# Hybrid diffusion step on one core: the Fourier product's exit from PSUM, its gate loads and weight sums, and the place of one product

## The chip, the cores and the metric

The kernel runs on one core of one Trainium2 chip. A core has five engines that run on their own instruction streams: TensorE (PE, matmuls), VectorE (DVE), ScalarE (ACT), GpSimd (POOL) and SyncE (SP, which here issues DMAs). The metric is the device time of the whole kernel in microseconds (us). Before the change its median is 1737.0 us over three runs (1736.28 to 1737.26).

## What is computed

One layer of a hybrid backbone over 1152 tokens: 128 of a context pass and 1024 of a denoising pass on a 16 x 64 grid, with 1024 channels and fp32 inputs. Cut to what the change touches, and then to what follows:

```python
h = rmsnorm(x, norm1_g) * (1.0 + scale1) + shift1
z = h @ w_in + b_in                      # columns: x_r, y_r, x_f (512), gates g_a and g_b
x_r = depthwise_conv(x_r, conv_w, conv_b)
rec = rglru_bidir(x_r, ...)              # per direction: r, i = sigmoid(...); a = exp(...);
                                         # b = sqrt(1 - a*a) * (i * x); h = scan(a, b)
out_a = (rec * gelu(y_r)) @ w_lru_out
out_b = fourier_mix(x_f) @ w_fnet_out    # real part of a DFT over positions and 64 group channels
mixed = (sigmoid(g_a) * out_a + sigmoid(g_b) * out_b) @ w_out
x = x + gate1 * mixed                    # then a second norm, SwiGLU and a final norm
```

Every product of fp32 numbers is made of three fp32r matmuls: both operands are split into a rounded high part and the rest, and high x high, high x low and low x high are summed in PSUM.

## The kernel before

The tokens lie along the free dimension. A weight step (`zstep`) is one 128-channel block of a product: 8 blocks of the contraction, three passes, three pieces of 384 columns, 72 matmuls. Its weights come in one DMA of 128 x 1024 into a raw tile (three exist), are split by an ACT cast (L207) and a DVE subtraction (L208), and are used by PE at L242. A list of steps is made by hand (L1301 to L1430); a loop (L1568 to L1597) runs them one after the other. For each step it issues the next step's own loads (`pre`), then weight DMAs and weight splits up to the step's own and `cap` further ones, the step's matmuls, then as many of the waiting background tasks as a running count of ACT's and DVE's work allows, and last the step's own work on its result (`post`, `after`). All engines take their instructions in the order of this recording, and SP its DMAs too, at most eight of them in flight.

The stages that matter here:

- Eight y_r steps, three of the sixteen gate products, then four heads. A head h is two x_r steps, a gate product, the four recurrence gates of block 2h (18 matmuls each, a sigmoid on ACT at L503), another gate product, and the four gates of block 2h + 1. A gate product ends in one sigmoid (L392) and a spill to memory by POOL (L393): the first eight make `sgb_d` (gates of the Fourier branch), the others `sga_d`. A block's recurrence is a list of background tasks: exponential (L527) and tanh (L530) on ACT, products on DVE and POOL (L533, L537, L540), square root on ACT (L543), scans on DVE, and a store of the result to `p_d`. Exponential, square root and sigmoid need different activation tables, so `ACT_TABLE_LOAD` stands between them. Z, the PSUM pool of these steps, has two buffers.
- x_f in two halves of 256 channels (216 matmuls each, L613 to L615), with a gate product between them. Each half leaves PSUM by five bias additions on DVE (L624).
- Four last gate products (`tail`), with the matmuls of the position DFT woven between their own (L647 to L731). `nyq_before` (L752 to L764), run at the second of them, clears a tile on POOL, loads the weights for the Nyquist row and splits them.
- The Fourier product (`ob_steps`), eight blocks m in two parts each. Weight blocks are first summed (`ob_item`, L789 to L793). The even part's result is copied by ACT to `eb` (L823); the odd part adds to it in the same PSUM buffer, of which there are three. `post_o` then makes from both the direct rows (even plus odd) and the mirrored rows (twice even minus the whole), each at once multiplied with the gate tile `ld` read back from `sgb_d` (L771), and stores `gbob`.
- `oa`, the product with w_lru_out: 72 matmuls per step on p, which is read back from `p_d` (L871) and split by `p_tasks` into `phi` (ACT, L246) and `plo` (DVE, L247). The first of these steps is the first that needs all eight blocks of p.

Of the kernel before, what the change touches and what calls it, by code (L numbers as in the profile page):

```python
# [14 lines left out]
ALU = mybir.AluOpType  # L15
# [3 lines left out]
P = 128  # L19
D = 1024  # L20
KD = D // P
LAT = 1024
CTX = 128
# [5 lines left out]
NW = 33  # L29
NC = 34  # L30
C2 = 2 * NC
NF = 8 * NW + NC
# [27 lines left out]
def kernel(ctx: ExitStack, tc: tile.TileContext, xT, vecs, cbc, bfb, ada1, ada2, w_in, w_xf, gatew,  # L60
                         w_lru, w_fnet, w_fnq, w_out, w_uv, w_ff, w_ff2, dftc, dftx, identd, y_out, st_out):
    nc = tc.nc
    nc_v, nc_a, nc_p, nc_t, nc_s = nc.vector, nc.scalar, nc.gpsimd, nc.tensor, nc.sync
# [37 lines left out]
    def TT(name, dt=F32, shape=(P, T)):  # L101
        t = tp.tile(list(shape), dt, name=name, tag="T")
        held.append(t)
        return t

    def LL(name, shape=(P, T)):
        return lp.tile(list(shape), F32, name=name, tag="L")
# [13 lines left out]
    sgb_d = dr.tile([KD, P, T], F32, name="sgb_d")  # L121
# [77 lines left out]
    cost = {"A": 0.0, "D": 0.0}  # L199
# [28 lines left out]
    woven = []  # L228
# [354 lines left out]
    fx = {}  # L583
    F = {}
    fhi, flo = [None] * 4, [None] * 4
    nyq = {}
# [11 lines left out]
    def xf_step(hf):  # L598
        box = {}

        def pe(hl):
            zs = [Z(), Z()]
            box["zs"] = zs
            for t in range(9):
                weave()
                ps = zs[t // 6][:, (t % 6) // 2, (t % 2) * 256:(t % 2) * 256 + 256]
                for k in range(KD):
                    hl_k = hl[k // 4]
                    rh = hl_k[:, 0, (k % 4) * 256:(k % 4) * 256 + 256]
                    rl = hl_k[:, 1, (k % 4) * 256:(k % 4) * 256 + 256]  # L610

                    th, tl = hhi[k][:, t * P:(t + 1) * P], hlo[k][:, t * P:(t + 1) * P]
                    nc_t.matmul(ps, th, rh, start=(k == 0), stop=False)  # L613
                    nc_t.matmul(ps, th, rl, start=False, stop=False)
                    nc_t.matmul(ps, tl, rh, start=False, stop=(k == KD - 1))  # L615

        def post():
            xs = [TT(f"X{hf}{q}", shape=(P, 4, 256)) for q in range(3)]
            fx["X", hf] = xs
            bias = fx["dx"][:, None, 456 + 256 * hf:712 + 256 * hf]  # L620
            for t in range(0, 9, 2):
                n = 2 if t < 8 else 1
                z = box["zs"][t // 6][:, (t % 6) // 2, :n * 256].rearrange("p (a b) -> p a b", a=n)
                nc_v.tensor_add(xs[t // 4][:, t % 4:t % 4 + n, :], z, bias.to_broadcast([P, n, 256]))  # L624
            cost["D"] += 3.5
            box.clear()

        return Step(23.5, pe, post, [w_xf[hf, 0], w_xf[hf, 1]], before=xf_before if hf == 0 else None)


# [121 lines left out]
    def nyq_before():  # L752
        nyq["x"] = TT("nqx", F32R, (P, 2, NF))
        nyq["f"] = TT("nqf", F32, (P, 2, NF))
        nc_p.memset(nyq["f"][:72], 0.0)
        r = LL("nqr", (P, 1024))
        nc_p.memset(r[:72], 0.0)
        for o in (0, 32, 64):
            nc_s.dma_start(r[o:o + 8], w_fnq)
        w = nyq["w"] = TT("nqw", F32R, (P, 1024))  # L760
        nc_a.copy(w[:72], r[:72])
        nc_v.tensor_sub(w[64:72], r[64:72], w[64:72].bitcast(F32))
        cost["A"] += 1.1
        cost["D"] += 1.2  # L764


    lbox = {}

    def load_l(key, src, new=None):
        t = (new or LL)("ld")  # L770
        nc_s.dma_start(t[:], src)  # L771
        lbox[key] = t
# [26 lines left out]
    def ob_steps(m):  # L799

        box = {}

        def part(odd, hl):
            w = ob_op[m // 2]
            ps = box["ps"]
            for k in range(2):
                for i, (we, x_) in enumerate(((0, fhi), (0, flo), (1, fhi))):
                    o = (m % 2) * 512 + odd * 256 + k * P
                    for c in range(2):
                        nc_t.matmul(ps[:, c, :NF], w[:, we, o:o + P], x_[2 * k + odd][:, c, :],  # L810
                                    start=(not odd and k == 0 and i == 0), stop=(odd == 1 and k == 1 and i == 2),
                                    skip_group_check=odd == 1)

        def pe_e(hl):
            box["ps"] = G()
            part(0, hl)
            for c in range(2):
                nc_t.matmul(box["ps"][:, c, :NF], nyq["w"][:72, m * P:(m + 1) * P], nyq["x"][:72, c, :], start=False,
                            stop=True)

        def post_e():
            box["e"] = TT("eb", shape=(P, 2, NF))
            nc_a.copy(box["e"], box["ps"][:, :2, :NF])  # L823
            cost["A"] += 0.8

        def pe_o(hl):
            part(1, hl)
            if m % 2 == 1:
                del ob_op[m // 2]
            if m == KD - 1:  # L830
                fhi.clear()
                flo.clear()
                nyq.clear()

        def post_o():
            g = TT("gbob")
            s = lbox.pop(("sgb", m))
            ps, eb = box["ps"], box["e"]
            half = lambda t: t[:, :LAT].rearrange("p (h r w) -> p h r w", h=2, w=64)
            rows = lambda t: t[:, :2, :8 * NW].rearrange("p h (r w) -> p h r w", w=NW)  # L840
            ctx_ = lambda t: t[:, :2, 8 * NW:NF]
            n = LAT + C2
            d = TT("df", shape=(P, 16 * NW + C2))
            nc_v.scalar_tensor_tensor(d[:, :16 * NW].rearrange("p (h n) -> p h n", h=2), eb[:, :, :8 * NW], 2.0,
                                      ps[:, :2, :8 * NW], op0=ALU.mult, op1=ALU.subtract)
            nc_v.scalar_tensor_tensor(d[:, 16 * NW:].rearrange("p (h n) -> p h n", h=2), ctx_(eb), 2.0, ctx_(ps),
                                      op0=ALU.mult, op1=ALU.subtract)
            for h in range(2):
                nc_v.tensor_mul(half(g)[:, h, :, 0:NW], rows(ps)[:, h], half(s)[:, h, :, 0:NW])
            nc_v.tensor_mul(g[:, LAT:n].rearrange("p (h n) -> p h n", h=2), ctx_(ps),  # L850
                            s[:, LAT:n].rearrange("p (h n) -> p h n", h=2))
            dv = d[:, :16 * NW].rearrange("p (r w) -> p r w", w=NW)[:, :, 1:32]
            grid = lambda t: t[:, :LAT].rearrange("p (r w) -> p r w", w=64)
            g3, s3 = grid(g), grid(s)
            nc_v.tensor_mul(g3[:, 15:0:-1, 63:32:-1], dv[:, 1:16, :], s3[:, 15:0:-1, 63:32:-1])
            nc_v.tensor_mul(g3[:, 0:1, 63:32:-1], dv[:, 0:1, :], s3[:, 0:1, 63:32:-1])
            k = CTX - C2
            nc_v.tensor_mul(g[:, n:][:, ::-1], d[:, 16 * NW + 1:16 * NW + 1 + k], s[:, n:][:, ::-1])
            nc_p.dma_start(gbob_d[m], g[:])
            cost["D"] += 3.2  # L860
            box.clear()

        return (Step(1.95, pe_e, post_e, [ob_item(m), ob_item(m + 1)] if m % 2 == 0 else []),
                Step(1.65, pe_o, post_o, pre=lambda: load_l(("sgb", m), sgb_d[m], TT)))

    phi, plo = [None] * KD, [None] * KD

    def p_tasks():
        def f(k):
            t = TT("pl")  # L870
            nc_s.dma_start(t[:], p_d[k])  # L871
            lbox["p", k] = t

        def g(k):
            if k + 1 < KD:
                f(k + 1)
            phi[k] = TT(f"phi{k}", F32R)
            plo[k] = TT(f"plo{k}", F32R)
            split(lbox.pop(("p", k)), phi[k], plo[k], nc_a.copy)
        return [((lambda: f(0)), 0, 0)] + [((lambda k=k: g(k)), 1.2, 1.4) for k in range(KD)]  # L880


    mx = [[None] * KD, [None] * KD]
# [417 lines left out]
    steps = []  # L1301
# [5 lines left out]

    def g():
        return gs.pop(0)
    steps += [g() for _ in range(3)]  # L1310
    for hd in range(4):
        steps.append(zstep(w_in[2 * hd], xr_post, 2 * hd))
        steps.append(zstep(w_in[2 * hd + 1], xr_post, 2 * hd + 1))
# [6 lines left out]
    db = [dft_b(ct) for ct in range(4)]  # L1320
    dc = [[dft_c(pair, odd) for odd in range(2)] for pair in range(2)]
    one = lambda fs: [[f] for f in fs]
    steps += [xf0, g(), xf1]
    xf1.before = lambda: woven.extend(one(da[0] + da[1][:4]))
    tail = gs[:]
    gs.clear()
    tail[0].before = lambda: woven.extend([[da[1][4], db[0][0]]] + one(db[0][1:] + db[1] + da[2][:2]))
    tail[1].before = lambda: (nyq_before(), woven.extend(one(da[2][2:4]) + [[da[2][4], da[3][0]]] + one(da[3][1:4])
                                                         + [[da[3][4], dc[0][0][0]], [dc[0][0][1]]]))
    tail[2].before = lambda: woven.extend(one(dc[0][1] + db[2] + db[3]))  # L1330
    tail[3].before = lambda: woven.extend(one(dc[1][0] + dc[1][1]))
    steps += tail
# [1 line left out]
    ob[0][0].before = lambda: (open_pool("z", ("psg0", 3), space=PSUM), drain())  # L1334
    pt = [f for f, _, _ in p_tasks()]
    ob[5][0].after = pt[0]
    for m in range(KD):
        ob[m][0].cap = 2
        if m > 4:
            ob[m][1].after = pt[m - 4]  # L1340
    steps.append(ob[0][0])
# [356 lines left out]
```

## Time and profile before

| | |
|---|---|
| median of three runs | 1737.0 us |
| the profiled execution | 1734.3 us |
| its span, first to last instruction | 1732.2 us |
| mean granted TensorE clock | 0.981 |
| PE busy | 1654.1 us (95%) |
| DVE busy | 1029.3 us (59%) |
| ACT busy | 594.0 us (34%) |
| POOL busy | 115.8 us (7%) |

The span leaves out some 2 us of the execution that lie around the first and last instruction. Since PE is busy for 95% of it, the time hangs on the few places where PE stands still and on the clock behind them: the granted clock is 1.0 at 2.4 GHz and 0.5 at 1.2 GHz, and a figure between is the mean of a stretch. Positions in the trace are microseconds from the span's start.

### The profile page before, as it was taken

The page shows a single profiled execution, that of the slowest core. Times are in us where ns is not written, and L with a number is a line of the kernel's source. Part 1 is how long each engine was busy: PE and PEld are TensorE (multiplying, and loading weights), DVE is VectorE, ACT ScalarE, POOL GpSimd, SP SyncE. Part 2 cuts the span into 40 slices and gives each one's busy share as a digit, 9 for nine tenths or more (in the row PEclk, how much of TensorE's full clock was granted, in tenths as well). Part 3 has the DMA queues.
Part 4 walks back from the last instruction along what each step waited for, and adds up shares of the span by engine and source line. Part 5 has one row for each costly group of instructions (what it writes and reads, how often), then busy time and mean ns, then how long its engine had stood idle before and what let it go on. Part 6 is the DMA issues. An engine that isn't in the chain of part 4 may idle for free.

```text
span 1732.2 us, 25391 instructions
## 1 busy us (share of the span) xinstructions
PE 1654.1 (95%) x10680; PEld 1622.3 (94%) x10680; DVE 1029.3 (59%) x1466; ACT 594.0 (34%) x758; POOL 115.8 (7%) x161
## 2 busy tenths in 40 slices
PE   6899999899999899699998799999999999999997
PEld 4799999899999899699998799999999999999997
DVE  6678966798775225534456766555555566444446
ACT  6482225665572222311235422222222232111112
POOL 0200001101010000000000000000000000000012
PEclk9999999999999999899999899999999999999999
DMA  9038731322241106743433132222222227222203
GB/s 368 13 100 310 239 111 66 104 78 78 90 151 66 53 33 235 293 145 117 155 121 113 61 104 95 77 70 77 77 77 77 77 71 283 82 81 100 92 12 110
DMA packets 56481, 201.88 MB, mean 117 GB/s; under 512 B 6640, under 2 KB 9088, under 8 KB 56368
## 3 DMA queue, kind: packets, MB, share of 16 engines
q1 hardware_dynamic: 45776, 158.96, 27.2%
q0 software_dynamic: 10592, 41.30, 6.3%
q8 instruction: 84, 1.38, 0.3%
q14 instruction: 29, 0.24, 0.0%
HBM read 154.17 MB, written 46.01 MB: 116 GB/s over the span
## 4 chain that ended last, share of the span: by engine, by line
PE 65%; issue 6%; DVE 4%; ACT 2%; DMA 2%; POOL 0%; SPq 0%; DVEq 0%; ACTq 0%; POOLq 0%
PE g L933 31%; PE z L242 30%; PE z L1273 3%; DMA pl<-p_d 1%; DMA ld<-sgb_d 1%; ACT x L1015 0%; DVE x L968 0%; DVE x L1010 0%; DVE ho L1094 0%; ACT b L1022 0%; DVE tlo L247 0%; DVE yt L1296 0%; PE a L681 0%; ACT hl L207 0%; ACT hl L792 0%
## 5 line engine op out<-in xcount | busy, mean ns | idle before, releaser
L242 PE MATMUL z<-hhi,hl 128*128 128x384 f32 x1344 | 282.2, 341 | 0.0
L933 PE MATMUL g<-thi,ho 128*128 128x288 f32 x1408 | 251.4, 296 | 0.0
L242 PEld LDWEIGHTS z<-hhi,hl 128*128 128x128 f32 x1344 | 238.8, 189 | 0.8 <-issue 0.8
L933 PE MATMUL g<-b,ho 128*128 128x288 f32 x1584 | 222.3, 299 | 16.1 <-ACT w L1149 12.2
L933 PEld LDWEIGHTS g<-b,ho 128*128 128x128 f32 x1584 | 216.7, 191 | 17.3 <-ACT w L1149 12.9
L933 PEld LDWEIGHTS g<-thi,ho 128*128 128x128 f32 x1408 | 209.3, 189 | 0.0
L242 PE MATMUL z<-shi,hl 128*128 128x384 f32 x864 | 175.6, 338 | 0.9 <-DVE w L1179 0.9
L208 DVE TENSOR_TENSOR hl<-wr,hl 128x1024 fp32r<-128x1024 f32 x86 | 104.6, 1222 | 92.1 <-ACT hl L207 91.4
L207 ACT CAST hl<-wr 128x1024 fp32r<-128x1024 f32 x86 | 89.3, 1042 | 191.9 <-PE z L242 170.1
L242 PE MATMUL z<-hlo,hl 128*128 128x384 f32 x672 | 155.0, 339 | 0.0
L242 PEld LDWEIGHTS z<-shi,hl 128*128 128x128 f32 x864 | 153.7, 188 | 1.1 <-issue 1.1
L933 PE MATMUL g<-tlo,ho 128*128 128x288 f32 x704 | 151.3, 296 | 0.0
L242 PEld LDWEIGHTS z<-hlo,hl 128*128 128x128 f32 x672 | 121.2, 188 | 0.0
L1093 ACT CAST ho<-wr 128x512 fp32r<-128x512 f32 x110 | 64.6, 618 | 159.8 <-DVE wr L1103 141.9
L1094 DVE TENSOR_TENSOR ho<-wr,ho 128x512 fp32r<-128x512 f32 x110 | 75.4, 687 | 67.5 <-ACT ho L1093 67.5
L933 PEld LDWEIGHTS g<-tlo,ho 128*128 128x128 f32 x704 | 113.2, 189 | 0.0
L912 DVE SCALAR_TENSOR_TENSOR x<-z,mods,x 128x768 f32<-128x768 f32 x40 | 40.7, 1018 | 115.4 <-PE z L242 115.4
L933 PE MATMUL g<-mx,hl 128*128 128x288 f32 x768 | 101.6, 294 | 0.0
L933 PEld LDWEIGHTS g<-mx,hl 128*128 128x128 f32 x768 | 101.1, 188 | 0.0
L242 PE MATMUL z<-slo,hl 128*128 128x384 f32 x432 | 99.3, 338 | 0.0
L242 PE MATMUL z<-phi,hl 128*128 128x384 f32 x384 | 81.4, 348 | 13.0 <-DVE gbob L850 7.8
L242 PE MATMUL z<-xchi,hl 128*128 128x384 f32 x384 | 80.8, 342 | 7.9 <-ACT g L503 7.9
(256 smaller groups left out, 2519.9 us busy)
## 6 DMA issues: line engine op xcount, KB each, us to landing
wr<-in_w_uv_dram SPq DMA_DIRECT2D x50, 512.0 KB, 3.6
wr<-in_w_in_dram SPq DMA_DIRECT2D x32, 512.0 KB, 3.7
adar<-in_ada_dram SPq DMA_DIRECT2D x32, 512.0 KB, 5.1
s_d<-w POOLq DMA_DIRECT2D x44, 288.0 KB, 2.4
sld<-s_d SPq DMA_DIRECT2D x22, 576.0 KB, 4.8
wr<-in_w_ff_dram SPq DMA_DIRECT2D x22, 512.0 KB
ada<-in_ada_dram SPq DMA_DIRECT2D x16, 512.0 KB, 9.7
wr<-in_w_out_dram SPq DMA_DIRECT2D x13, 512.0 KB, 4.9
```

Of the source, the lines that this page charges most:

```text
L207: nc_a.copy(h[:, 0], r)
L208: nc_v.tensor_sub(h[:, 1], r, h[:, 0].bitcast(F32))
L242: nc_t.matmul(ps[:, c, :CH], w, xx[:, c * CH:(c + 1) * CH], start=(k == first and i == 0), stop=(k == last and i == 2))
L912: nc_v.scalar_tensor_tensor(dst[:, :768].rearrange("p (c n) -> p c n", c=2), ps[:, 0:2, :CH], mods[:, gq, 0, m:m + 1], src[:, :768].rearra ...
L933: nc_t.matmul(ps[:, c, :HC], w(e, k), xx[:, c * HC:(c + 1) * HC], start=(first and i == 0 and j == 0), stop=(last and i == len(ks) - 1 and ...
L1093: nc_a.copy(h[:, 0], src)
L1094: nc_v.tensor_sub(h[:, 1], src, h[:, 0].bitcast(F32))
L1273: nc_t.matmul(ps[:, b, :hi - lo], ww, xx[:, lo:hi], start=(j == js[0] and i == 0), stop=(j == js[-1] and i == 2))
```

## The change

It has four parts.

1. The list of steps begins with four gate products where it had three, and none stands between the halves of x_f any more. Three of a half's five bias additions are issued after its sixth group of matmuls, not after its last.
2. The Nyquist tile is cleared and loaded in `tail[0]`; its split becomes `nyq_weights`, woven in as the last piece of `tail[1]`.
3. `post_o` copies the direct rows from PSUM to `gbob` on ACT, makes the mirrored rows in `gbob` by five combinations on DVE, and multiplies the whole tile (1152 elements) with the gate tile in SBUF.
4. Gate loads are issued two to three blocks ahead, p loads two ahead, and `cap` is 4 at `tail[3]` and at the first two blocks (2 before).

```diff
+                if t == 5:
+                    out(range(0, 6, 2))
+        def out(ts):
+            if "X" not in box:
+                box["X"] = fx["X", hf] = [TT(f"X{hf}{q}", shape=(P, 4, 256)) for q in range(3)]
...
-            for t in range(0, 9, 2):
+            for t in ts:
...
+        def post():
+            out((6, 8))
...
-        r = LL("nqr", (P, 1024))
+        r = nyq["r"] = LL("nqr", (P, 1024))
         nc_p.memset(r[:72], 0.0)
         for o in (0, 32, 64):
             nc_s.dma_start(r[o:o + 8], w_fnq)
+
+    def nyq_weights():
+        r = nyq.pop("r")
         w = nyq["w"] = TT("nqw", F32R, (P, 1024))
...
-            s = lbox.pop(("sgb", m))
+            sb = lbox.pop(("sgb", m))
...
+            nc_a.copy(g[:, :LAT].rearrange("p (h r w) -> p h r w", h=2, w=64)[:, :, :, 0:NW], rows)
+            nc_a.copy(g[:, LAT:n].rearrange("p (h n) -> p h n", h=2), ps[:, :2, 8 * NW:NF])
+
+            g3 = g[:, :LAT].rearrange("p (r w) -> p r w", w=64)
+            for h, r0, r1, to in ((0, 1, 8, slice(15, 8, -1)), (1, 0, 8, slice(8, 0, -1)), (0, 0, 1, slice(0, 1))):
+                nc_v.scalar_tensor_tensor(g3[:, to, 63:32:-1], er[:, h, r0:r1, 1:32], 2.0, rows[:, h, r0:r1, 1:32],
+                                          op0=ALU.mult, op1=ALU.subtract)
+            gx = g[:, LAT:]
+            for h, a, b in ((0, 1, NC), (1, NC, CTX - C2 + 1)):
+                o = 8 * NW - h * NC
+                nc_v.scalar_tensor_tensor(gx[:, CTX - a:CTX - b:-1], eb[:, h, o + a:o + b], 2.0, ps[:, h, o + a:o + b],
+                                          op0=ALU.mult, op1=ALU.subtract)
+            nc_v.tensor_mul(g, g, sb)
...
-            if k + 1 < KD:
-                f(k + 1)
+            if k + 2 < KD:
+                f(k + 2)
...
-    steps += [g() for _ in range(3)]
+    steps += [g() for _ in range(4)]
...
-    steps += [xf0, g(), xf1]
+    steps += [xf0, xf1]
...
+    tail[3].cap = 4
+    ob[0][0].pre = lambda: sgb_load(0, 1, 2)
     for m in range(KD):
-        ob[m][0].cap = 2
+        ob[m][0].cap = 4 if m < 2 else 2
+        if 0 < m < 6:
+            ob[m][0].pre = lambda m=m: sgb_load(m + 2)
```

Part 1 also changes which background tasks the loop puts between the steps. On ACT, at head 1, before (`g_0_2160` and `g_2_2212` are the previous block's r of both directions, `g_0_2570` to `g_3_2653` the gates of this one):

```order
L392 ACT_TABLE_LOAD
L392 ACTIVATE sg<-z,vec 128x1152
L207 CAST hl<-wr 128x1024
L503 ACTIVATE g_0_2570<-z,vec 128x1152
L543 ACT_TABLE_LOAD
L543 ACTIVATE g_0_2160<-g_0_2160 128x1152
L543 ACTIVATE g_2_2212<-g_2_2212 128x1152
L503 ACT_TABLE_LOAD
L503 ACTIVATE g_1_2611<-z,vec 128x1152
L503 ACTIVATE g_2_2632<-z,vec 128x1152
L503 ACTIVATE g_3_2653<-z,vec 128x1152
```

and after, at the same head, with the gate product between its two blocks (`g_0_2671` and `g_2_2713` of the first block, `g_0_2870` to `g_3_2933` the gates of the second):

```order
L543 ACT_TABLE_LOAD
L543 ACTIVATE g_0_2671<-g_0_2671 128x1152
L543 ACTIVATE g_2_2713<-g_2_2713 128x1152
L392 ACT_TABLE_LOAD
L392 ACTIVATE sg<-z,vec 128x1152
L207 CAST hl<-wr 128x1024
L503 ACTIVATE g_0_2870<-z,vec 128x1152
L503 ACTIVATE g_1_2891<-z,vec 128x1152
L503 ACTIVATE g_2_2912<-z,vec 128x1152
L503 ACTIVATE g_3_2933<-z,vec 128x1152
```

The square roots (L543) moved from between two sigmoids of the gates to ahead of the gate product's sigmoid (L392); all four heads have the second form now, and before the last two had it.

On POOL, from the last store of p to the first stores of the Fourier product, before:

```order
L566 DMA p_d<-sq_4049 128x1152
L393 DMA sga_d<-sg 128x1152 x2
L755 MEMSET nqf 72x596
L757 MEMSET nqr 72x1024
L393 DMA sga_d<-sg 128x1152 x3
L859 DMA gbob_d<-gbob 128x1152 x8
```

and after (L761 and L763 are the same two lines):

```order
L566 DMA p_d<-sq_4130 128x1152
L761 MEMSET nqf 72x596
L763 MEMSET nqr 72x1024
L393 DMA sga_d<-sg 128x1152 x4
L864 DMA gbob_d<-gbob 128x1152 x8
```

The two clearings moved ahead of the spills of the tail's gate products, which wait for ACT.

On SP, around the Fourier product, before, from the first gate load on:

```order
L771 DMA ld<-sgb_d 128x1152 x2
L782 DMA wr<-in_w_fnet_dram 128x1024 x2
L771 DMA ld<-sgb_d 128x1152 x2
L196 DMA wr<-in_w_lru_dram 128x1024 x2
L771 DMA ld<-sgb_d 128x1152
L871 DMA pl<-p_d 128x1152
L771 DMA ld<-sgb_d 128x1152
L196 DMA wr<-in_w_lru_dram 128x1024 x2
L871 DMA pl<-p_d 128x1152
L771 DMA ld<-sgb_d 128x1152 x2
L871 DMA pl<-p_d 128x1152
```

and after, likewise:

```order
L780 DMA ld<-sgb_d 128x1152 x3
L791 DMA wr<-in_w_fnet_dram 128x1024 x3
L740 DMA nqf<-F 4x596 x3
L780 DMA ld<-sgb_d 128x1152
L791 DMA wr<-in_w_fnet_dram 128x1024 x2
L780 DMA ld<-sgb_d 128x1152 x3
L196 DMA wr<-in_w_lru_dram 128x1024 x2
L780 DMA ld<-sgb_d 128x1152
L881 DMA pl<-p_d 128x1152 x2
L196 DMA wr<-in_w_lru_dram 128x1024 x2
L881 DMA pl<-p_d 128x1152 x2
```

Seven of the eight gate loads moved ahead of the first w_lru load, where four stood, and p's first two loads ahead of the second pair of w_lru.

## Rows read from the trace of the kernel before

**Rows 1.** Waits of PE: engine, line, waited for: total us, times, longest
```profile
PE z L242 <- ACT g L503: 7.9, 2, 6.3
PE z L242 <- DVE gbob L850: 7.8, 1, 7.8
PE a L659 <- DVE u L652: 5.2, 1, 5.2
PE z L242 <- ACT phi L246: 5.2, 2, 4.0
```

**Rows 2.** Timeline of ACT, head 1: start, us, engine, line, instruction, idle before
```profile
321.85 2.43 ACT L543 ACTIVATE g<-g 128x1152 f32<-128x1152 f32 x2 [5.10 <-DVE g L540]
...
325.60 2.33 ACT L503 ACTIVATE g<-z,vec 128x1152 f32<-128x1152 f32 x2
```

**Rows 3.** Timeline of ACT, head 2, the gate product between its blocks
```profile
409.47 1.22 ACT L503 ACTIVATE g<-z,vec 128x1152 f32<-128x1152 f32 x1 [1.94 <-PE z L242]
...
422.36 1.28 ACT L392 ACT_TABLE_LOAD   x1
423.66 1.23 ACT L392 ACTIVATE sg<-z,vec 128x1152 f32<-128x1152 f32 x1
```

**Rows 4.** Timeline of PE, the same place
```profile
424.54 1.23 PE L242 MATMUL z<-xchi,hl 128*128 128x384 f32 x6
```

**Rows 5.** Windows: length, busy us (instructions) by engine, granted clock, DMA share, GB/s
```profile
326.87:331.56 4.69, 4.69 (x19) 4.69 (x19) 4.59 (x7) 1.06 (x1) 0.00 (x0) 0.66 0.00 0
607.78:614.75 6.97, 6.97 (x28) 6.97 (x29) 1.25 (x4) 0.77 (x2) 0.00 (x0) 0.60 0.00 0
650.00:660.00 10.00, 10.00 (x68) 9.70 (x68) 2.74 (x9) 1.77 (x3) 0.00 (x0) 1.00 0.05 21
710.00:720.00 10.00, 5.28 (x22) 3.81 (x20) 3.89 (x4) 1.15 (x1) 0.53 (x1) 0.79 1.02 419
```

**Rows 6.** Timelines of POOL, SP and ACT, the Nyquist weights
```profile
600.11 0.53 POOL L393 DMA_DIRECT2D sga_d<-sg  x1 [48.95 <-ACT sg L392]
...
601.16 0.98 POOL L757 MEMSET nqr<- 72x1024 f32 x1
...
602.17 1.04 SPq L759 DMA_DIRECT2D nqr<-in_w_fnq_dram  x3
...
605.02 1.04 ACT L761 CAST nqw<-nqr 72x1024 fp32r<-72x1024 f32 x1 [4.27 <-DMA nqr<-in_w_fnq_dram]
```

**Rows 7.** Timelines of DVE and PE, end of x_f's first half, last tail step
```profile
536.44 1.02 DVE L624 TENSOR_TENSOR X<-z,dx 128x512 f32<-128x512 f32 x2 [1.14 <-PE z L615]
537.38 2.35 DVE L208 TENSOR_TENSOR hl<-wr,hl 128x1024 fp32r<-128x1024 f32 x2
...
648.82 0.42 DVE L706 COPY F<-a 128x256 f32<-128x256 f32 x1
...
652.38 0.38 PE L702 MATMUL a<-dc,va 128*128 128x128 f32 x2
```

**Rows 8.** Groups by line, 665 to 730: count, busy us, mean ns, idle before
```profile
L247 DVE TENSOR_TENSOR plo<-pl,phi 128x1152 fp32r<-128x1152 f32 x8 | 10.8, 1356 | 7.6 <-ACT phi L246 7.4
...
L844 DVE SCALAR_TENSOR_TENSOR df<-eb,g 128x528 f32<-128x528 f32 x8 | 5.6, 698 | 1.9 <-PE g L810 1.9
...
L823 ACT COPY eb<-g 128x596 f32<-128x596 f32 x8 | 4.9, 652 | 0.0
```

**Rows 9.** Timelines of PE, SP and ACT, from the Fourier product to `oa`
```profile
665.30 0.43 PE L810 MATMUL g<-fhi,hl 128*128 128x298 f32 x2
...
706.17 4.60 SPq L871 DMA_DIRECT2D pl<-p_d  x4
...
724.35 1.15 ACT L246 CAST phi<-pl 128x1152 fp32r<-128x1152 f32 x1 [0.19 <-DMA pl<-p_d]
...
729.53 1.22 PE L242 MATMUL z<-phi,hl 128*128 128x384 f32 x6
```

**Rows 10.** DMA issues, 600 to 732: count, KB each, median us to landing
```profile
pl<-p_d SPq DMA_DIRECT2D x8, 576.0 KB, 13.9
```

More of the change, by code (lines that the diff above doesn't have):

```diff
@@ L615, in pe @@
                     nc_t.matmul(ps, tl, rh, start=False, stop=(k == KD - 1))
-        def post():
-            xs = [TT(f"X{hf}{q}", shape=(P, 4, 256)) for q in range(3)]
-            fx["X", hf] = xs
+                if t == 5:
[3 more added lines that the diff above has]
+                box["X"] = fx["X", hf] = [TT(f"X{hf}{q}", shape=(P, 4, 256)) for q in range(3)]
+            xs = box["X"]
             bias = fx["dx"][:, None, 456 + 256 * hf:712 + 256 * hf]
-            for t in range(0, 9, 2):
+            for t in ts:
                 n = 2 if t < 8 else 1
@@ L624, in post @@
                 nc_v.tensor_add(xs[t // 4][:, t % 4:t % 4 + n, :], z, bias.to_broadcast([P, n, 256]))
-            cost["D"] += 3.5
+                cost["D"] += 0.7
+        def post():
+            out((6, 8))
             box.clear()
@@ L836, in post_o @@
             g = TT("gbob")
-            s = lbox.pop(("sgb", m))
+            sb = lbox.pop(("sgb", m))
             ps, eb = box["ps"], box["e"]
-            half = lambda t: t[:, :LAT].rearrange("p (h r w) -> p h r w", h=2, w=64)
-            rows = lambda t: t[:, :2, :8 * NW].rearrange("p h (r w) -> p h r w", w=NW)
-            ctx_ = lambda t: t[:, :2, 8 * NW:NF]
             n = LAT + C2
-            d = TT("df", shape=(P, 16 * NW + C2))
-            nc_v.scalar_tensor_tensor(d[:, :16 * NW].rearrange("p (h n) -> p h n", h=2), eb[:, :, :8 * NW], 2.0,
-                                      ps[:, :2, :8 * NW], op0=ALU.mult, op1=ALU.subtract)
@@ L846, in post_o @@
[L846 to L858, printed above, removed]
+            rows = ps[:, :2, :8 * NW].rearrange("p h (r w) -> p h r w", w=NW)
@@ new lines, in post_o @@
+            er = eb[:, :, :8 * NW].rearrange("p h (r w) -> p h r w", w=NW)
+            nc_a.copy(g[:, :LAT].rearrange("p (h r w) -> p h r w", h=2, w=64)[:, :, :, 0:NW], rows)
[4 more added lines that the diff above has]
+                                          op0=ALU.mult, op1=ALU.subtract)
@@ L859, in post_o @@
+            gx = g[:, LAT:]
[4 more added lines that the diff above has]
+            nc_v.tensor_mul(g, g, sb)
             nc_p.dma_start(gbob_d[m], g[:])
-            cost["D"] += 3.2
+            cost["A"] += 0.9
+            cost["D"] += 2.7
@@ L861, in post_o, with sgb_load @@
             box.clear()
         return (Step(1.95, pe_e, post_e, [ob_item(m), ob_item(m + 1)] if m % 2 == 0 else []),
-                Step(1.65, pe_o, post_o, pre=lambda: load_l(("sgb", m), sgb_d[m], TT)))
+                Step(1.65, pe_o, post_o))
+    def sgb_load(*ms):
+        for m in ms:
+            load_l(("sgb", m), sgb_d[m], TT)
     phi, plo = [None] * KD, [None] * KD
@@ L879, in g @@
             split(lbox.pop(("p", k)), phi[k], plo[k], nc_a.copy)
-        return [((lambda: f(0)), 0, 0)] + [((lambda k=k: g(k)), 1.2, 1.4) for k in range(KD)]
+        return [((lambda: (f(0), f(1))), 0, 0)] + [((lambda k=k: g(k)), 1.2, 1.4) for k in range(KD)]
     mx = [[None] * KD, [None] * KD]
@@ L1326 @@
     gs.clear()
-    tail[0].before = lambda: woven.extend([[da[1][4], db[0][0]]] + one(db[0][1:] + db[1] + da[2][:2]))
-    tail[1].before = lambda: (nyq_before(), woven.extend(one(da[2][2:4]) + [[da[2][4], da[3][0]]] + one(da[3][1:4])
-                                                         + [[da[3][4], dc[0][0][0]], [dc[0][0][1]]]))
+    tail[0].before = lambda: nyq_before() or woven.extend([[da[1][4], db[0][0]]] + one(db[0][1:] + db[1] + da[2][:2]))
+    tail[1].before = lambda: woven.extend(one(da[2][2:4]) + [[da[2][4], da[3][0]]] + one(da[3][1:4])
+                                                         + [[da[3][4], dc[0][0][0]], [dc[0][0][1], nyq_weights]])
     tail[2].before = lambda: woven.extend(one(dc[0][1] + db[2] + db[3]))
```

## The prediction

> **What bounds the kernel now.** The page's first part gives TensorE (PE) 95% of the span, so I looked only for stretches in which PE waits, and took each for itself. The waits by engine come first [rows 1]; four entries lie in the part that the change touches. PE waits 7.9 us in two times, the longer 6.3, for a gate sigmoid; 7.8 us for the multiplication that frees a Fourier buffer; 5.2 us for a copy behind the Nyquist weights; 5.2 us for the fp32r casts of the recurrence's result p. The timelines say what stood ahead of each. Then the windows [rows 5] show what a wait costs behind its end: the granted clock is 0.66 in the 4.69 us after the first and 0.60 in the 6.97 us after the third, averages of a part at 1.2 GHz and a part at 2.4 GHz, each time after PE had stood still for over 5 us.
>
> **A. Four products first, halves of x_f in a row.** The step that stood between the halves moves ahead of the recurrence; its 72 matmuls are the same work. What changes is the order that the planner makes on ScalarE (ACT). Before, square roots stand between the first and the second sigmoid of a block's gates. At the first such place they wait 5.10 us for VectorE (DVE), so the second sigmoid starts only at 325.60, and PE waits with it [rows 2]. In the new order they stand ahead of the product's own sigmoid, and the four gate sigmoids follow each other. The old kernel has this order already at heads 2 and 3, so the trace shows its price: last gate sigmoid at 409.47, table load at 422.36, product's sigmoid from 423.66 to 424.89 [rows 3], and PE goes through the six matmuls at 424.54, three for each of two buffers, without a wait [rows 4]. The second three start some 0.53 us in, at 425.07: a margin of 0.2 us.
> Gone are then 7.9 us of wait [rows 1] and the slow clock behind the long one, 4.69 x (1 - 0.66) = 1.6 us [rows 5]: 9.5. The new order comes to two more places, heads 0 and 1. At head 1 the queues ahead are those of heads 2 and 3, so nothing is added. At head 0 DVE also has ten additions and products of eight elements ahead, at most the fixed 0.14 us each that the price in C gives [rows 8], so a stall between nothing and 1.4 - 0.2 us; I take 0.5. **A = -9.0** (ends -6 and -9.5).
> All of this goes by ScalarE's rows, where a table load is 1.28 us [rows 3]. The Trainium skill, page "ScalarE: Activation LUTs", section "Rules for kernel authors", tells to budget about 2.7 us for every switch to another set. The chain holds three switches (exponential, square root, sigmoid); each 1.4 us longer, it would be some 4.0 us late at each new place, A would be -9.5 + 8.0 = -1.5, and the sum 1719. The row speaks against it.
>
> **B. Nyquist weights.** PE's wait of 5.2 us [rows 1] ends a chain on three queues [rows 6]: GpSimd (POOL) clears the tile at 601.16, behind a spill that itself waited for ACT until 600.11; SyncE (SP) issues the three loads only at 602.17; ACT's cast starts at 605.02, and DVE's subtraction and copies follow. Now the clearing stands ahead of that spill, in the step before, and the loads with it, a whole product's time earlier; cast and subtraction are issued last among the woven pieces, behind the copies that PE waits for. What covers them is the rest of that step and the next. Gone: 5.2 + 6.97 x (1 - 0.60) = 2.8. **B = -7.9** (ends -8, and -6 if the two instructions still hold up a copy).
>
> **E. Second half's weights.** Without a step between the halves, the split of its second half-weight has no cover. In the trace DVE's last two bias additions begin at 536.44 upon PE's last matmul and take 1.02 us, and a subtraction is half of 2.35 [rows 7]; so the low part would be there about 2.2 us after the first half's end. PE asks for it 13 matmuls in, of 256 columns at the pace of [rows 4] (0.53 us for three of 384): 1.5 us. The change issues the other three additions within the half, which keeps them out of this chain. **E = +0.6** (0 to 2).
>
> **D. Last tail step.** With its look-ahead raised to 4, three weight sums are prepared ahead of the Fourier copies. The copy that started at 648.82 on DVE then stands behind three times two sums of 256 and a subtraction of 512 elements, 0.4 + 0.4 + 0.7 us by the price below, and ends near 653.2; PE's next group at 652.38 needs its buffer [rows 7]. **D = +0.8** (0 to 2).
>
> **C. From the Fourier product to the next stage.** S is the product's first matmul, 665.30; the last cast of p starts at 724.35, S+59, 0.19 us after its load, and the first p-step ends near 730.1, S+64.8, with the first three of the matmuls at 729.53 [rows 9]. DMA sets this end: in 710 to 720 the engines are busy 1.02 of the time at 419 GB/s, while in 650 to 660 they were busy 0.05 [rows 5]. The four last p loads were issued at 706.17 and over 4.60 us [rows 9].
> PSUM first. The product now leaves it by two ACT copies and five DVE combinations; the gate load is wanted only by one multiplication in SBUF. A DVE instruction costs 0.14 us plus 1.05 ns an element (0.698 us for 528, 1.356 for 1152 [rows 8]). Before: eight instructions, 1748 elements, 3.0 us a block. After: six, 1708 elements, 2.6 us. ACT gets some 0.6 + 0.25 us more a block, by its copy of 596 in 0.652 [rows 8], and DVE waits for it; three PSUM buffers hide that, but in the middle, where sums stand ahead, I count 1.5 us on PE. It replaces waits of the same size, so the stage stays at some 32 us. The 7.8 us go [rows 1], but PE then only comes to p earlier, and p's loads are late next.
> Loads next. Seven of eight gate loads stand ahead of the first w_lru load, in the idle stretch or right at S. SP then stops at the second w_lru load until a raw tile is free, behind the third block on DVE: an estimate of S+17, four blocks of 32 us / 8. From there to the last p load there are one gate load, eight of p, four for the next stage and five stores of 0.59 MB, and three weights of 0.52: 12.2 MB, 29 us at 419 GB/s, so S+46, and S+48.5 with the landing. ACT's cast and DVE's of 1.36 us [rows 8] and the rest of the matmuls give the first p-step's end at S+55.2. **C = -9.6.** Ends: -3 if SP is held some 7 us longer, -15 if the last load lands by S+43.
>
> **Sum.** -9.0 - 7.9 + 0.6 + 0.8 - 9.6 = -25.1. The profiled execution took 1734.3 us, which would become 1709.2; from the median of the runs, 1737.0, it is 1711.9.
>
> **Rivals.**
> 1. *The loads stay the bound.* The bytes are the same, the engines are full in the end, and the in-order SP queue can hold p behind w_lru. Against it: seven gate loads of 1.4 us each (0.59 MB at 419 GB/s) leave the full stretch. If it holds, C is -3: 1718.5.
> 2. *The recurrence's wait only moves.* The margin is 0.2 us, and head 0 has more on DVE. Each us on DVE is one of PE at two places; 3.5 us late at both gives A = -2.5: 1718.4. Against it: two places ran so without a wait [rows 4].
> 3. *More is won.* The last p lands by S+43: C = -15, 1706.5.
> 4. *Slower.* A task that casts p(k) issues the load of p(k+2), so two are ahead. If that ties issue to landing, the loads go in four pairs of 13.9 us [rows 10], the last landing at S+17 + 56 = S+73, 14 us later than before. With PE idle far longer, the first p-step runs at 1.2 GHz for another 5: C = +19, sum +3.5: 1740.5. It decides once landing and clock together are 15.5 us later than before. Against it: before, with one ahead, four loads were issued in 4.60 us [rows 9], so the issue did not follow the casts one by one.
> 5. *It does not do what it says*: the Nyquist wait stays because cast and subtraction come late all the same: 1719.8.
>
> **How the numbers follow.** Forecast 0.62, rivals 0.16, 0.08, 0.06, 0.06 and 0.02. A measurement here tells 0.2%, 3.5 us, from no change. Rivals 1 to 3 and 5 are all faster; of rival 4 I put a third within 0.2% (the pairs without the clock's loss, sum -1.5) and two thirds beyond: faster 0.94, same 0.02, slower 0.04. The range takes in the ends of A to E and rivals 1, 2, 3 and 5, and leaves out rival 4 and the corners where several ends meet: 1705 to 1724.
>
> **What will show it.** PE's waits for the gate sigmoid and for the copy at 602 gone, and the granted clock behind them at 1.0; the wait for the Fourier buffer (7.8) gone; last cast of p at about S+50; new waits of half a microsecond to one and a half at the second half of x_f, in the last tail step and in the middle of the Fourier product. Wrong would be a wait in heads 0 and 1 at the product's sigmoid, or a last p landing after S+56.

## The result, and the profile after

The changed kernel takes 1715.2 us (median of four runs, 1714.6 to 1717.9), the kernel before 1736.6 beside it: -21.4 us, ratio 0.9881 with a 95% interval of 0.9864 to 0.9898 (-18 to -24 us). Forecast were -25.1 us, 1711.9, within 1705 to 1724. A second measurement of both gave 0.9882. Seven single runs of the measurements below, one of them of the kernel before, were 9 to 13 us shorter than the median of the rest of their set, for no reason that was found; times are therefore medians, and the ratios, which such runs pull along, differ a little from them.

Where PE waits, by the waits of the changed kernel (engine, line, waited for: total us, times, longest), the entries that answer to [rows 1] and to the new waits of the forecast:

```profile
PE z L242 <- ACT phi L246: 5.1, 2, 3.0
...
PE z L242 <- DVE plo L247: 3.1, 4, 1.7
PE g L819 <- ACT eb L832: 2.5, 3, 1.7
...
PE z L242 <- DVE gbob L861: 1.2, 1, 1.2
...
PE a L708 <- DVE F L712: 0.8, 1, 0.8
...
PE z L242 <- ACT sg L392: 0.6, 1, 0.6
PE z L614 <- DVE hl L208: 0.3, 1, 0.3
```

The gate sigmoid's 7.9 us and the 5.2 behind the Nyquist weights have no entry any more; the Fourier buffer's 7.8 has become 1.2. The casts of p (phi and plo) now cost 8.2 us, where they cost 5.2 and 0.9 before: PE comes to them earlier and waits there.

The windows of the changed kernel (columns as in [rows 5]): head 0, the end of head 1, the tail steps with the Nyquist weights, the stretch from the end of SP's stop (SP standing at a weight load that waits for a free tile) to the last cast of p, and a window across the end of that stretch:

```profile
270.00:280.00 10.00, 9.39 (x54) 9.06 (x53) 9.89 (x9) 7.49 (x7) 0.00 (x0) 1.00 0.00 0
320.00:330.00 10.00, 10.00 (x59) 10.00 (x58) 9.74 (x9) 3.39 (x3) 1.00 (x2) 1.00 0.16 55
...
600.00:610.00 10.00, 10.00 (x73) 9.72 (x72) 3.08 (x8) 3.27 (x5) 0.00 (x0) 1.00 0.00 0
...
667.70:703.20 35.50, 24.18 (x134) 20.76 (x132) 24.77 (x43) 17.17 (x26) 2.67 (x5) 0.91 0.97 375
...
700.00:710.00 10.00, 8.18 (x32) 7.67 (x33) 4.59 (x4) 3.46 (x3) 0.00 (x0) 0.65 0.22 89
```

PE is full in 320 to 330 and 600 to 610, and the granted clock, 0.66 and 0.60 behind the two waits before [rows 5], is 1.00. What is left of the slow clock around here lies behind the waits for p: 0.84 in 690 to 700, 0.65 in 700 to 710.

To lay the traces side by side I use five marks in each: S, the Fourier product's first matmul; the last cast of p; the first post-operation of the next stage; the first matmul of the residual product; and that of the SwiGLU stage on the second half of the tokens. Times are us.

| kernel | S | S to last p cast | S to first post-operation | residual product to SwiGLU | median of runs |
|---|---|---|---|---|---|
| before | 665.3 | 59.1 | 65.0 | 164.7 | 1736.6 |
| after | 649.7 | 53.7 | 59.7 | 166.4 | 1715.2 |

Up to S the change wins 15.6 us, where A, B, E and D together had been put at 15.5. So close an agreement is luck: S lies between 649.0 and 651.2 in the eight traces, the changed kernel's among them, of kernels whose code up to S is that of the changed kernel, so one trace tells it to some 2 us. From S to the first post-operation the change wins 5.2 (64.96 against 59.74), where C had been put at 9.6. Then 1.7 are lost in a stretch that the change does not touch. In all the two traced executions differ by 19.0 us (1734.3 and 1715.3), the medians by 21.4; the executions of the kernel before counted so far lay between 1734.3 and 1737.3.

### The profile page after: what moved, and what is told of

It is laid out like the page before. It is cut to its first block, busy times and chain, and to the rows that moved or that the text cites. A ratio compares the mean times of both kernels' runs of the same rounds, so it can differ in the third digit from the quotient of the medians.

```text
span 1713.4 us, 25413 instructions
## 1 busy us (share of the span) xinstructions
PE 1650.7 (96%) x10680; PEld 1618.7 (94%) x10680; DVE 1029.1 (60%) x1450; ACT 598.2 (35%) x773; POOL 118.4 (7%) x161
## 4 chain that ended last, share of the span: by engine, by line
PE 75%; DVE 4%; issue 3%; ACT 2%; DMA 2%; POOL 0%; DVEq 0%; SPq 0%; POOLq 0%; ACTq 0%
PE z L242 35%; PE g L943 31%; PE z L1283 3%; DMA pl<-p_d 1%; PE z L614 1%; PE z L613 1%; PE z L615 1%; PE a L687 1%; PE g L819 0%; DVE hl L208 0%; ACT x L1025 0%; PE a L653 0%; DVE x L978 0%; DVE x L1020 0%; ACT b L1032 0%
## 5 line engine op out<-in xcount | busy, mean ns | idle before, releaser
L943 PEld LDWEIGHTS g<-b,ho 128*128 128x128 f32 x1584 | 217.5, 192 | 17.8 <-ACT w L1159 13.0
L421 DVE SCALAR_TENSOR_TENSOR junk<-adar,cb 128x1024 f32<-128x1024 f32 x64 | 78.3, 1224 | 5.0 <-DMA adar<-in_ada_dram 3.1
```

The source lines that it names most:

```text
L421: nc_v.scalar_tensor_tensor(env["j"], w, 1.0, env["c"][v], op0=ALU.mult, op1=ALU.mult, accum_out=out[:, v:v + 1])
L943: nc_t.matmul(ps[:, c, :HC], w(e, k), xx[:, c * HC:(c + 1) * HC], start=(first and i == 0 and j == 0), stop=(last and i == len(ks) - 1 and ...
```

## Experiments

The first question was whether the parts stand for themselves; the second, why C was half of what I had worked out.

### One part at a time

Part 1 alone is the kernel before with

```diff
-    steps += [g() for _ in range(3)]
+    steps += [g() for _ in range(4)]
...
-    steps += [xf0, g(), xf1]
+    steps += [xf0, xf1]
```

and the split bias additions. 

> Only part 1 on the kernel before: four gate products first, the halves of x_f in a row, three additions within the half. My theory (the gate sigmoids' wait and the clock behind it go, nothing takes their place): -9.5 +0.6 at head 0 +0.3 at the second half of x_f = -8.6, so 1728 for 1737; PE's waits for the gate sigmoid 0, one wait of some 0.6 for the product's sigmoid at head 0, granted clock 1.0 between 270 and 500. Rival (the wait only moves to the product's sigmoid at several heads): within 2 us of 1737, with waits of 3 us or more in two heads.

Measured: 1726.3 for 1734.8, ratio 0.9942 (0.9925 to 0.9958). S comes at 656.4, 8.9 earlier, and the stretch behind S is as before (65.1 for 65.0). PE's waits in heads and x_f are the two expected ones, 0.6 at the product's sigmoid of head 0 and 0.3 at the second half of x_f. The timeline of ACT in this kernel shows the 0.6:

```profile
270.83 2.44 ACT L543 ACTIVATE g<-g 128x1152 f32<-128x1152 f32 x2 [1.91 <-DVE g L540]
273.29 1.28 ACT L392 ACT_TABLE_LOAD   x1
274.59 1.22 ACT L392 ACTIVATE sg<-z,vec 128x1152 f32<-128x1152 f32 x1
```

At head 2 of the kernel before, the place that [rows 3] show, the square root waited 0.96 us for DVE:

```profile
419.90 2.44 ACT L543 ACTIVATE g<-g 128x1152 f32<-128x1152 f32 x2 [0.96 <-DVE g L540]
```

At head 0 it waits 1.91, so it is 0.95 later, and less the margin of 0.2 that is about the 0.6.

Part 2 alone:

```diff
-    tail[1].before = lambda: (nyq_before(), woven.extend(...
+    tail[0].before = lambda: nyq_before() or woven.extend(...
+    ... [dc[0][0][1], nyq_weights]
```

> Only part 2 on the kernel before: the Nyquist weights cleared and loaded one step earlier, split as the last woven piece. My theory: the wait of 5.2 and the slow clock behind it, 2.8, go together: -7.9, 1729; no wait at that place, clock 1.0 there. Rival (only the wait goes, the clock stays lower for another reason): -5.2, 1732. Rival (the split holds up the copies instead): under -3, 1734 or more.

Measured: 1728.0, ratio 0.9951 (0.9934 to 0.9969). S comes at 658.0, 7.3 earlier, though this execution was 0.7 late already when the heads ended (last gate matmul at 511.1 for 510.4), so the part won 8.0 in its place. No wait is left in 590 to 612 and the windows there show 1.00. Wait and clock went together.

Parts 3 and 4 alone, the new exit, loads and look-ahead. 

> Only parts 3 and 4 on the kernel before: the new exit from PSUM, the gate and p loads further ahead, more weight sums ahead. By the trace of the changed kernel its share is +0.8 at the last tail step and -5.2 from the Fourier product to the end of the first p-step: -4.4, 1732.6. By my blind forecast it would be -8.8, 1728. Rival (this stage gains only because its loads start later or earlier beside the other parts): between -2 and +2.

Measured: 1732.4, ratio 0.9977 (0.9964 to 0.9989), -2 to -6 us. From S to the first post-operation 59.3 for 65.0: the -5.2 of the changed kernel's trace does not hang on the other parts. The last tail step waits 0.8, as there. S itself comes 3.1 later in this trace (668.4); of that 1.5 stood already at the end of the heads, which this kernel leaves as they were, 0.8 is the wait, and the rest is open.

The changed kernel again. 

> The changed kernel again, for the sum of the three parts on the same chip: if the parts add up, -8.6 -7.9 -4.4 = -20.9, so 1716 for 1737; if they overlap, less than the three runs' sum by more than 3 us. Theory for the 1.7 us that the trace of the changed kernel loses between the first residual product and the SwiGLU products: chance of the clock's phase, so in this run between -1 and +2 against the kernel before; if it is an effect of the change, again 1.5 to 2.

Measured: 1714.5, ratio 0.9882 (0.9869 to 0.9895), -20.3 us. The three parts give -10.1, -8.5 and -4.0 by their ratios, -22.6 in sum, and -8.6, -6.8 and -2.4 by the medians, -17.8: the whole lies between. The stretch from the residual product to SwiGLU took 166.5 here. It also took 166.6 in the kernel with part 1 alone, whose code and neighbours there are those of the kernel before, and 165.9 with part 2 alone; over all thirteen later traces 165.0 to 166.8. So I take 164.7, of which there is one trace, as a short draw of the kernel before, and the 1.7 us as no effect of the change. What differs between draws was not tested.

### Exit or loads?

Two kernels each undo one side of what was done at the Fourier product. The first has the loads of before, and with them the look-ahead of before:

```diff
-                Step(1.65, pe_o, post_o))
+                Step(1.65, pe_o, post_o, pre=lambda: sgb_load(m)))
...
-            if k + 2 < KD:
-                f(k + 2)
+            if k + 1 < KD:
+                f(k + 1)
...
-    tail[3].cap = 4
...
-        ob[m][0].cap = 4 if m < 2 else 2
...
+        ob[m][0].cap = 2
```

> The changed kernel with the loads and look-ahead of before (gate loads block by block, p one ahead, look-ahead 2), and the new exit from PSUM kept. From the product's first matmul S to the first post-operation of the next stage: 65.0 before, 59.7 in the changed kernel. Theory (what the loads must carry after S sets that end): about 65, so 5 slower than the changed kernel, and 0.8 won back at the last tail step: some 1719. PE then comes to p early, but waits for p all the longer; no wait for the Fourier buffer. Rival (the exit itself gives the gain): about 60, some 1714.

The second has the `post_o` of before. 

> The changed kernel with the exit from PSUM of before (eight DVE instructions that read PSUM and the gate tile), and the new loads and look-ahead kept. Theory: the gate tiles are there in time, so the old exit does not hold PSUM; S to the first post-operation about 60, as in the changed kernel, total some 1714.5. Rival (the exit was needed): 65 or more, 1720.

Measured: 1720.9 (ratio 0.9921, 0.9897 to 0.9944) and 1715.6 (0.9888, 0.9867 to 0.9910). From S to the first post-operation:

| | loads and look-ahead of before | new loads and look-ahead |
|---|---|---|
| exit of before | 65.0 | 59.0 |
| new exit | 67.2 | 59.7 |

Loads and look-ahead together give all of it; which of the two gives how much is not shown, since no kernel undoes the look-ahead with the new loads kept. The new exit alone makes the stretch 2.2 longer: PE's waits with the old loads and the new exit are

```profile
PE z L242 <- ACT phi L246: 7.0, 3, 3.9
PE z L242 <- DVE plo L247: 4.6, 3, 3.7
PE g L819 <- ACT eb L832: 4.3, 4, 1.8
PE z L242 <- DVE gbob L861: 1.3, 1, 1.3
```

The 7.8 us of the Fourier buffer are gone without the new loads, but PE then stands before p, whose last cast comes at S+61.0 for S+59.1. With the new loads and the old exit that wait is 2.4 us and not 7.8:

```profile
PE z L242 <- ACT phi L246: 4.9, 2, 2.9
PE z L242 <- DVE plo L247: 2.8, 3, 1.6
PE z L242 <- DVE gbob L859: 2.4, 1, 2.4
PE g L819 <- ACT eb L832: 1.6, 2, 1.0
```

The gate tiles are there in time: DVE's multiplications of the direct rows stood idle 5.3 us for them in the kernel before, and not at all in this one (groups by line, before and this kernel):

```profile
L849 DVE TENSOR_TENSOR gbob<-g,ld 128x264 f32<-128x264 f32 x16 | 6.2, 427 | 5.3 <-DMA ld<-sgb_d 5.3
```

```profile
L858 DVE TENSOR_TENSOR gbob<-g,ld 128x264 f32<-128x264 f32 x16 | 6.1, 426 | 0.0
```

### What bounds the loads?

If C fell short because of the bytes that had to pass ahead of the last p load, then four loads that nobody needs yet should be moved behind it:

```diff
-    oa[0].before = lambda: ([f() for f in pt[4:]], open_pool(...
+    oa_pre = [oa[m].pre for m in range(2)]
+    oa[0].pre = oa[1].pre = None
+    oa[0].before = lambda: ([f() for f in pt[4:]], [f() for f in oa_pre], open_pool(...
```

> The changed kernel with the four loads of the next stage's first two steps (two gates, two Fourier products, 2.36 MB, 5.6 us at 419 GB/s) issued behind the last p load, not among them. Theory (bytes behind SP's stop): the last p cast starts at S+48 for S+53.5, the first post-operation at S+55 for S+59.7, so some 1710; the four loads then land about 6 us later, just in time for the two post-operations. Rival (the stop of SP and the order of casts set the end, not bytes): last cast at S+53 still, 1714.5. Rival (the four loads become late in turn): last cast early, first post-operation not, 1714.

Measured: 1707.6, ratio 0.9832 (0.9803 to 0.9861), 7 us under the changed kernel. Last cast at S+47.6, first post-operation at S+51.8 for S+59.7. That is 8 us for 5.6 us of bytes. The windows from S to that mark, of the changed kernel and of this one, show the rest:

```profile
649.70:709.40 59.70, 47.81 (x282) 44.15 (x282) 37.23 (x69) 25.72 (x40) 4.80 (x9) 0.91 0.78 299
```

```profile
651.00:702.70 51.70, 44.20 (x283) 41.23 (x282) 37.15 (x69) 25.62 (x40) 4.79 (x9) 1.00 0.89 343
```

The same matmuls kept PE busy for 47.8 us at a mean clock of 0.91 and for 44.2 at 1.00. Of the 8 us, 3.6 are the clock and 4.4 are waits (59.7 - 47.8 against 51.7 - 44.2). The two long waits for p (3.0 and 2.1) are gone in this kernel, and the clock did not fall.

The same, with `ob[2][0].after = pt[0]` for `ob[5][0].after = pt[0]`, so that two p loads stand ahead of the w_lru loads. 

> As the one before, and the first two p loads issued ahead of the first w_lru loads, that is before SP stops and while the DMA engines are half idle. Theory: another 1.2 MB leave the full stretch, 2.8 us: last cast at S+45.5, where DVE's own work (casts behind the exit) sets the end at about S+53: some 1708. Rival (SP's stop sets the end): 1714.5 as without.

Measured: 1707.6, ratio 0.9846 (0.9823 to 0.9869); last cast at S+47.2, post-operation at S+51.3. The cast came 0.4 and the end 0.5 earlier, though 2.8 us of loads were to leave the stretch. SP's timeline says why: the other six p loads still stand behind SP's second stop, which ended at 676.64, 27.6 after S:

```profile
668.64 8.00 SPq L196 DMA_DIRECT2D wr<-in_w_lru_dram  x2
676.75 1.59 SPq L881 DMA_DIRECT2D pl<-p_d  x3
```

With four p loads early and always four ahead (`f(0)` to `f(3)` at first, `f(k + 4)` in `g(k)`): 

> As the run with p first and two p loads early, but four p loads ahead of the first w_lru loads and always four ahead. Theory (two p loads early gave 0.5 because the last six were still issued when SP's second stop ended, 27.7 after S): now four are left behind that stop, 1.2 MB less, 2.8 us: last cast at S+44.5 for S+47.3, first post-operation at S+49 for S+51.3, some 1705. Rival (DVE's own chain is the bound by now: it was busy 0.99 of 680 to 690): S+51 again, 1707.5. Rival (four loads before SP's first stop push the gate loads back): a wait for a gate tile, and later than S+52.

Measured: 1706.1, ratio 0.9814 (0.9793 to 0.9834); last cast at S+43.3, post-operation at S+49.7. The casts come 4 us earlier, the end 1.6, between the theory's S+49 and the rival's S+51. No wait of PE for phi is left, the largest sums being 2.5 for plo and 2.5 for `eb`. ACT waits 4.0 us for the last p load, but PE no longer stands behind it; PE's last wait is 0.55 for plo at 691.0. In 680 to 690 DVE is full, so that from here DVE's own work sets the end, as the rival had it:

```profile
680.00:690.00 10.00, 6.93 (x39) 6.07 (x38) 9.93 (x18) 7.96 (x9) 1.59 (x3) 1.00 1.01 378
```

### The exit again, and the look-ahead

With p first, the exit from PSUM might matter. 

> p first, as in the run that gave 1707.6, with the exit from PSUM of before. Theory (with the loads out of the way DVE sets the pace of the casts, and the old exit costs DVE 0.2 to 0.35 us more a block, with 0.85 less on ACT): the first post-operation 0 to 2 later than S+51.8, total 1707.5 to 1709.5. Rival (ACT was the crowded engine): up to 2 earlier, 1706.

> Four p loads early, as in the run that gave 1706.1, with the exit from PSUM of before. Theory (the exit is worth nothing once its gate tiles are early; DVE and ACT both have room enough): S to the first post-operation 49 to 50 as there, 1706. Rival (by now DVE sets the end, and the new exit's 0.3 us a block less on DVE shows): 51 to 52, 1708.

Measured: 1707.2 (ratio 0.9831, 0.9818 to 0.9845) and 1704.8 (0.9821, 0.9807 to 0.9834); post-operation at S+51.1 for S+51.8 and at S+49.2 for S+49.7. In the first I had expected the old exit to be up to 2 us later; it was 0.7 earlier, on the rival's side. In the second it makes next to no difference, as expected. In all three pairs with the new loads the stretch is 0.4 to 0.7 shorter with the old exit, where three traces with the new one differ by 0.4 among themselves (59.31 to 59.75); the medians do not tell the two apart. So the new exit gains nothing in any of the four pairs. The last kernel has the lowest median measured here, 31 us under the kernel before, and is as fast within its interval as the one with four p loads and the new exit.

Last, the raised look-ahead at the tail (`tail[3].cap = 4`) was taken out of the kernel with p first. 

> p first, without the raised look-ahead at the last tail step (two weight sums back behind the step). Theory: the wait of 0.8 in that step goes, S comes 0.8 earlier after the second half of x_f; the two sums then stand at the first blocks, where up to 0.8 can return as a wait: total -0.8 to 0, 1707. Rival (the sums were needed early): the first blocks wait more than 1 us, 1708 or more.

Measured: 1712.8, ratio 0.9863 (0.9848 to 0.9878), 5 us worse, as the rival had it. The 0.8 us wait in the tail is gone, and the first block of the Fourier product waits 4.7, because ACT's copy `eb` now stands behind four casts of sums, each 2 us behind the other. The first two blocks keep their look-ahead of 4 in this kernel, so that they ask for all four at once. Timeline of ACT in that kernel:

```profile
649.33 0.61 ACT L801 CAST hl<-fe 128x512 fp32r<-128x512 f32 x1
651.37 0.62 ACT L801 CAST hl<-fe 128x512 fp32r<-128x512 f32 x1 [1.43 <-DVE fe L799]
653.41 0.62 ACT L801 CAST hl<-fe 128x512 fp32r<-128x512 f32 x1 [1.43 <-DVE fe L799]
655.46 0.62 ACT L801 CAST hl<-fe 128x512 fp32r<-128x512 f32 x1 [1.43 <-DVE fe L799]
655.98 1.21 ACT L832 COPY eb<-g 128x596 f32<-128x596 f32 x2
```

## Why the prediction was right, and where not

**A, -9.0: right.** Both waits went, the new order ran at all four heads, and head 0 paid 0.6 where I had put 0.5. The margin read from head 2 of the kernel before was the argument that carried it. Among the signs of being wrong stood a wait at the product's sigmoid in heads 0 and 1; at head 0 it came, at the size that the sum had put there, so that sign was drawn too sharp. The 2.7 us a switch of the Trainium skill, page "ScalarE: Activation LUTs", section "Rules for kernel authors", would have made it -1.5 by the forecast's estimate. The trace does not agree: a table load took 1.28 us after as before, and in the rows of ACT above the whole switch, from the square root's end at 273.27 to the sigmoid's start at 274.59, took 1.3.

**B, -7.9: right.** -7.3 at S alone, 8.0 in its place; the clock's 2.8 went with the wait, as the windows show.

**E, +0.6: 0.3.** The row of the changed kernel has DVE's last two additions at 539.77 and the pair of subtractions done at 543.06; PE waited 0.26.

**D, +0.8: right in size, in part by luck.** The wait is 0.84 in the changed kernel. But three times 1.5 us, counted from 648.82, end at 653.3, and with its own 0.42 the copy would be done at 653.7, not 653.2. What happened instead: the kernel before already has one of the sums ahead of this copy, and the changed kernel two more, each 2.05 us long, because DVE waits for ACT's cast within it (DVE before, then after):

```profile
648.21 0.69 DVE L793 TENSOR_TENSOR hl<-fe,hl 128x512 fp32r<-128x512 f32 x1 [2.17 <-ACT hl L792]
```

```profile
633.57 0.69 DVE L802 TENSOR_TENSOR hl<-fe,hl 128x512 fp32r<-128x512 f32 x1 [0.68 <-ACT hl L801]
...
635.62 0.69 DVE L802 TENSOR_TENSOR hl<-fe,hl 128x512 fp32r<-128x512 f32 x1 [0.69 <-ACT hl L801]
636.22 0.42 DVE L712 COPY F<-a 128x256 f32<-128x256 f32 x1
```

What the look-ahead gives in return had no term. The last experiment does not price it: its 4.7 us come from raising the look-ahead at the first two blocks and not at the step ahead of them. With 2 at all of them, in the kernel with the loads of before, the first block waits as little as in the changed kernel (PE at that place, with the loads of before, in the changed kernel, and in the last experiment):

```profile
653.58 0.55 PE L819 MATMUL g<-fhi,hl 128*128 128x298 f32 x2 [0.57 <-ACT eb L832]
```

```profile
654.30 0.54 PE L819 MATMUL g<-fhi,hl 128*128 128x298 f32 x2 [0.57 <-ACT eb L832]
```

```profile
656.68 0.54 PE L819 MATMUL g<-fhi,hl 128*128 128x298 f32 x2 [4.66 <-ACT eb L832]
```

Over the whole product that kernel waits 4.3 us for `eb` where the changed kernel waits 2.5; its loads differ too, so what the raised look-ahead is worth stays open.

**C, -9.6: measured -5.2; this is the term that was mis-sized.** The mechanism held: PSUM comes free, PE only comes to p earlier, and the loads behind SP's stop set the end. SP's and ACT's timelines of the changed kernel:

```profile
653.07 14.55 SPq L196 DMA_DIRECT2D wr<-in_w_lru_dram  x2
667.71 0.38 SPq L780 DMA_DIRECT2D ld<-sgb_d  x1
668.14 1.86 SPq L881 DMA_DIRECT2D pl<-p_d  x2
670.10 7.25 SPq L196 DMA_DIRECT2D wr<-in_w_lru_dram  x2
...
685.01 4.78 SPq L881 DMA_DIRECT2D pl<-p_d  x3
...
703.39 1.15 ACT L246 CAST phi<-pl 128x1152 fp32r<-128x1152 f32 x1 [0.17 <-DMA pl<-p_d]
```

The stop ended at S+17.9, for S+17 in the forecast. From there to 703.2 the windows above give 35.5 us at 375 GB/s, 13.3 MB. I had 12.2 MB: the w_lru load that SP was stopped at was itself left out, and one of the stores. And I had taken 419 GB/s, the rate of one full window, for the whole stretch. The last p was there at S+53.5, not S+48.5 (and its cast at S+53.7), so the end came at S+59.7, not S+55.2. The way from the last load to the end took 6.2 us where the forecast had 6.7, with the slow clock (0.65 in 700 to 710) in it: the whole miss lies in the landing.

**The rivals.** That the loads stay the bound (C of -3, 0.16) had the right place, and the truth lies between it and the forecast. My argument against it counted seven gate loads out of the full stretch; but four of the eight stood ahead of the first w_lru load already, so three more left it, 4.2 us at the price used there, near the 5.2 that were won. That the recurrence's wait only moves did not happen, and neither did the other three.

**What I had argued and not shown.** I let the exit's speed stand beside the loads as if both mattered. Its price was right; the groups by line of the changed kernel (columns as in [rows 8]) are

```profile
L863 DVE TENSOR_TENSOR gbob<-gbob,ld 128x1152 f32<-128x1152 f32 x8 | 10.9, 1358 | 0.3
...
L856 DVE SCALAR_TENSOR_TENSOR gbob<-eb,g 128x248 f32<-128x248 f32 x8 | 3.2, 406 | 0.0
...
L851 ACT COPY gbob<-g 128x528 f32<-128x528 f32 x8 | 5.0, 622 | 4.6 <-PE g L819 4.3 <-ACT phi L246 0.4
...
L852 ACT COPY gbob<-g 128x68 f32<-128x68 f32 x8 | 1.8, 224 | 0.0
```

The two ACT copies take 0.62 + 0.22 us, for 0.6 + 0.25. The table of the four kernels with either exit says that only the loads, with the look-ahead, did. The forecast's own sum had given the exit no time, so the number did not suffer.

## What to carry to other kernels

Where an in-order queue stops for a buffer and a stage behind it is short of bytes, list what stands between the stop and the load that is needed first: moving four loads that were not yet needed behind it was worth 7 us, a third of the whole change, and freeing PSUM early was worth nothing, with p's loads late or early. Price a removed wait with the clock behind it (5.2 us of wait were 8.0 us here), and look for a place in the old trace that already has the new order before guessing at its cost. A look-ahead that is raised at one step and not at the step ahead of it puts all that it asks for in front of one copy (4.7 us of wait here); look at both steps together.

## What the runs showed of the hardware that was not expected

In stretches in which the DMA engines were busy all the time (share 1.01 or 1.02), the rate was not one number: 419 GB/s in 710 to 720 before and in 690 to 700 of the changed kernel, 390 in a 12.6 us window of the changed kernel with loads and stores mixed, and 381 in 19.4 us of the kernel with two p loads early:

```profile
677.40:690.00 12.60, 9.21 (x54) 8.04 (x53) 12.50 (x23) 8.30 (x13) 1.60 (x3) 1.00 1.02 390
```

```profile
676.70:696.10 19.40, 15.24 (x84) 13.15 (x83) 16.94 (x27) 11.68 (x16) 1.59 (x3) 1.00 1.01 381
```

That stores make the difference is a guess; no run here separates them.

The granted clock of the changed kernel behind its two long waits for p (2.98 us up to 696.01, and 2.07 up to 701.76) is, in windows of 2 us:

```profile
694.00:696.00 2.00, 0.00 (x0) 0.00 (x0) 0.01 (x1) 1.15 (x1) 0.00 (x0) 1.00 1.02 417
696.00:698.00 2.00, 1.40 (x5) 1.08 (x6) 1.35 (x1) 0.00 (x0) 0.00 (x0) 0.71 1.02 419
698.00:700.00 2.00, 1.69 (x6) 1.18 (x4) 0.00 (x0) 0.00 (x0) 0.00 (x0) 0.50 1.02 412
...
708.00:710.00 2.00, 2.00 (x14) 2.00 (x13) 0.55 (x1) 0.00 (x0) 0.00 (x0) 1.00 0.00 0
```

It had fallen to 0.50, which is 1.2 GHz, before the second wait began, and was back at 1.00 in 708 to 710. In the kernel with p first, whose waits there are of up to 1.7 us, it stayed at 1.00. That the wait of 2.98 us caused the fall is read from these two kernels alone.
